# An encoder layer on one core: the tiles that TensorE reads are given the lowest places in SBUF

## The chip, the cores and the metric

The kernel runs on one core of a Trainium2 chip. The metric is the device time of one execution in microseconds (us). Before the change the median of three runs was 736.91 us (736.8 to 738.08). One further execution was profiled; it took 736.86 us, of which 735.1 us lie between its first and its last instruction (the span).

## The reference

One layer over 256 tokens of width 1024, in float32. An RMS norm is followed by one wide projection, four branches (a gated linear recurrence, differential attention, latent attention, retention), a gated merge of the four, an output projection, a squared-ReLU feed-forward of width 4096, and a gated addition of a side input:

```
xn = rms_norm(x, norm1_g)
(a_x, a_g, b_q, b_k, b_v, c_q, c_kv, c_kpe, d_q, d_k, d_v, d_g, gate_logits) = split(xn @ w_in)
y_a, y_b, y_c, y_d = the four branches
gates  = sigmoid(gate_logits + gate_b)
merged = gates[0]*(y_a @ w_br_a) + gates[1]*(y_b @ w_br_b) + gates[2]*(y_c @ w_br_c) + gates[3]*(y_d @ w_br_d)
x = x + merged @ w_out
x = x + square(relu(rms_norm(x, norm2_g) @ w_ff1)) @ w_ff2
x = x + sigmoid(rms_norm(x, norm3_g) @ w_ple_gate) * (p @ w_ple_proj)
```

## The kernel before

**Split products.** Every large product is made of three products of a reduced float32 format (F32R): each operand is split into a high part (a rounded copy) and a low part (the rest), and high by high, high by low and low by high are summed in PSUM (`a_mm`, `mm3`). ScalarE makes the high part and VectorE the low part.

**Weights.** Weight blocks of up to 1 MB are loaded by DMA from the SP queue into three buffers `raw` of 8 KB a partition (`load`, L361). `pieces` (L370) splits them into `hi` and `lo`, each a ring of five buffers of 4 KB a partition (NR = 5). From there TensorE reads them.

**Two forms of product.** In the a form (`a_mode`, L394) the activations are the stationary operand (128x128) and the weights are streamed, 512 columns at a time: `xTh`, `xTl` (the normed input, transposed and split), `y` (the split branch outputs), `h` (the split feed-forward activations), `cT` and `pT` are stationary there. A block of 1024 rows and 512 columns takes 48 matmuls, 24 for each half of the weights. In the b form (`b_mode`, L427) the weights are stationary and 256 columns of `xTh`, `xTl` are streamed; it makes the two inputs of the recurrence and the first feed-forward product. All of these are issued from one line, L194 (`mm`); transposes against the identity come from L207.

**Branch outputs.** `y4()` (L463) hands out the buffers of the split outputs: eight buffers of 4 KB a partition (NY = 8), tile name `y` in the profile. They hold the four branches' outputs in turn (read by `merge`, 96 matmuls for each of the four), the merged sum (read by the `w_out` product, 96 matmuls), the first half of the feed-forward activations (tiles 0 to 7 of 16, read by the `w_ff2` product, 192 matmuls), and at last the weights of the first 512 columns of `w_ple_gate`, where they are the streamed operand against a stationary `xTh` or `xTl` (48 matmuls). The other half of the feed-forward activations lies in the pools `L` and `SH` (tile name `h`).

**Order.** The code is laid out stage by stage; small generators (`side`, `tick`) put the attention and recurrence steps between blocks of the large products, and the tile framework sets the order on each engine from that. The last stages are `merge` of the fourth branch, `w_out`, `w_ple_proj`, 16 blocks of `w_ff1`, `w_ff2`, and the ple gate, which goes over two token halves t and inside each over two column halves c (0: weights in `y`, 1: weights in `hi`, `lo`).

**Places in SBUF.** A pool gets its place when it is opened, one behind the other from 16 KB of each partition on (below that lies a reserved area). Within a pool the tiles follow in the order of their first use. Where the tiles lie, in KB from the start of a partition, as the built program has them:

| tile | before | after |
|---|---|---|
| ident | 29.1 | 16.1 |
| xTh, xTl | 32.4 to 48.4 | 16.6 to 32.6 |
| hi | 73.2 to 93.2 | 32.6 to 52.6 |
| lo | 93.2 to 113.2 | 52.6 to 72.6 |
| y (eight buffers) | 183.2 to 215.2 | 72.6 to 104.6 |
| xs (rows of the input, later the sum) | 16.1 to 24.1 | 104.6 to 112.6 |
| par and other constants | 24.1 to 32.4, 48.4 to 49.2 | 112.6 to 121.2 |
| raw (three buffers) | 49.2 to 73.2 | 121.2 to 145.2 |
| small | 113.2 to 115.2 | 145.2 to 147.2 |
| SH (attention scratch, h 14 and 15, pT) | 115.2 to 147.2 | 147.2 to 179.2 |
| L (attention operands, h 8 to 13, cT) | 147.2 to 183.2 | 179.2 to 215.2 |
| gate | 215.2 to 223.2 | 215.2 to 223.2 |

Before, `ident`, `xs`, `xTh`, `hi`, `lo` and `raw` start at multiples of 64 bytes, and `y`, `SH`, `L` and `gate` at 32 bytes past one. After, `ident`, `xTh`, `xTl`, `hi`, `lo` and `y` start at multiples of 128 bytes; `SH`, `L` and `gate` are still 32 bytes past a multiple of 64.

Of the kernel before, what the change touches and what calls it, by code (L numbers as in the profile page):

```python
# [8 lines left out]
F32 = mybir.dt.float32  # L9
F32R = mybir.dt.float32r  # L10
# [4 lines left out]
P = 128  # L15
S = 256
# [4 lines left out]
NR, NY, NG, NL, NS = 5, 8, 4, 18, 16  # L21
# [146 lines left out]
def encoder_kernel(ctx: ExitStack, tc: tile.TileContext, a, out):  # L168
    nc = tc.nc
    MULT, ADD, SUB, MAX = ALU.mult, ALU.add, ALU.subtract, ALU.max  # L170

    const = ctx.enter_context(tc.tile_pool(name="const", bufs=1))
    ring = ctx.enter_context(tc.tile_pool(name="ring", bufs=4))
    psacc = ctx.enter_context(tc.tile_pool(name="psacc", bufs=4, space=bass.MemoryType.PSUM))
    psmm = ctx.enter_context(tc.tile_pool(name="psmm", bufs=4, space=bass.MemoryType.PSUM))
    small = ctx.enter_context(tc.tile_pool(name="small", bufs=4))
# [49 lines left out]
                nc.sync.dma_start(xs[:, t, w], a['x'][0, t * P:(t + 1) * P, w])  # L226
        nc.sync.dma_start(par[:, :O_LATE], a['params'][:, :O_LATE])

    ident = const.tile([P, P], F32, name="ident")
    make_identity(nc, ident)  # L230
    eps = const.tile([P, 3], F32, name="eps")
    for j, v in enumerate((EPS, 1e-33)):
# [61 lines left out]
        return nhalf[:, :2 * n].rearrange("p (t n) -> p t n", t=2)  # L294


    xTh = const.tile([P, 8, S], F32R, name="xTh")
    xTl = const.tile([P, 8, S], F32R, name="xTl")

    def rstd(src, scratch):  # L300

# [59 lines left out]
    def load(name, r0, n0):  # L361
        o, (_, _, rows, _, nn, mode) = offs[name, r0, n0]
        sz = rows * nn // P
        raw = ring.tile([P, 2048], F32, tag="raw", name="raw", bufs=3)
        with tc.high_priority(AHEAD):
            nc.sync.dma_start(raw[:, :sz], a['weights'][o:o + rows * nn].rearrange("(p c) -> p c", c=sz))
        return raw
# [23 lines left out]
    def a_mode(xh, xl, name, KT, n0, nn, by_token=0):  # L391


        ps = [acc_bank()[:, :nn] for _ in range(2)]  # L394
        held = []
        for k0 in range(0, KT, 4):
            kc = min(4, KT - k0)
            raw = load(name, k0 * P, n0)
            for p0 in range(0, kc, 2):
                kp = min(2, kc - p0)  # L400
                hi, lo = pieces(raw, p0 * nn, kp * nn)
                late = k0 >= KT - by_token
                for t in range(2):
                    for j in range(kp):
                        k = k0 + p0 + j
                        args = (ps[t], t, xh, xl, k, hi, lo, slice(j * nn, (j + 1) * nn), k == 0, k == KT - 1)
                        if late and t == 1:
                            held.append(args)
                        else:
                            a_mm(*args)  # L410
            tick(kc * nn / 2048)
        if held:
            yield ps[0]
            for args in held:
                a_mm(*args)
            yield ps[1]
        else:
            yield ps
# [4 lines left out]
    def b_mode(xh, xl, name, n0):  # L423

        ps = acc_bank().rearrange("p (f s) -> p f s", s=S)
        raw = load(name, 0, n0)
        for f in range(2):  # L427
            hi, lo = pieces(raw, f * 1024, 1024)
            for k in range(8):
                w = slice(k * P, (k + 1) * P)  # L430
                mm(ps[:, f, :], hi[:, w], xh(k), k == 0, False)
                mm(ps[:, f, :], hi[:, w], xl(k), False, False)
                mm(ps[:, f, :], lo[:, w], xh(k), False, k == 7)
        tick(1)
        return ps
# [5 lines left out]
    with tc.tile_pool(name="br", bufs=1) as br:  # L441
# [19 lines left out]
                    split_scaled(xTh[:, kk, :], xTl[:, kk, :], pt[:, k, :], c1('norm1_g', kk))  # L461

        def y4():  # L463
            return br.tile([P, 4, S], F32R, tag="y4", name="y4", bufs=NY)

        def yhl():

            return [[y4(), y4()] for _ in range(2)]
# [554 lines left out]
        for f2 in range(16):  # L1023
            ps = b_mode(xh, xl, 'w_ff1', f2 * 256)
            rl = br.tile([P, 512], F32, tag="gate", name="rl", bufs=NG)
            act(rl, ps.rearrange("p f s -> p (f s)"), AF.Relu)
            tt(rl, rl, rl, MULT)
            if f2 < 8:
                if f2 % 2 == 0:
                    h2 = [x.rearrange("p k s -> p (k s)") for x in (y4(), y4())]  # L1030
                hT.append([x[:, 512 * (f2 % 2):512 * (f2 % 2) + 512] for x in h2])
            elif f2 < 14:
                hT.append([L("h", F32R), L("h", F32R)])
            else:
                hT.append([SH("h").bitcast(F32R), SH("h").bitcast(F32R)])
            split(hT[f2][0], hT[f2][1], rl)
# [14 lines left out]
        for c in range(2):  # L1051
            alloc = (lambda: y4().rearrange("p k s -> p (k s)")) if c == 0 else None
            for k0 in (0, 4):
                raw = load('w_ple_gate', k0 * P, 512 * c)
                held += [pieces(raw, p0 * 512, 1024, alloc) for p0 in (0, 2)]
# [36 lines left out]
```

## Time and profile before

| | |
|---|---|
| median of three runs | 736.91 us |
| profiled execution | 736.86 us |
| its span | 735.1 us |
| TensorE (PE) busy | 718.0 us, 98% of the span, 4066 matmuls |
| weight loads (PEld) busy | 622.7 us, 85% |
| VectorE (DVE) busy | 526.6 us, 72% |
| ScalarE (ACT) busy | 428.2 us, 58% |
| HBM read | 126.74 MB |
| granted TensorE clock | 1.0 |

PE is TensorE's matmuls, PEld its weight loads, which run beside the matmuls. A matmul's row in the profile has a modelled end, so that the rows of neighbours overlap; the pace of a stream of matmuls is read from their starts. In the timeline a row gives the start, the length, the engine, the line, and the tiles written and read; a row x2 is two instructions merged. In the group rows the columns are the line, engine and operation, the tiles out<-in, the shape, the count, the busy time in us, the mean of one in ns, and the idle time of the engine ahead of them.

### The profile page before, as it was taken

How to read it: one execution, taken by the hardware profiler on the slowest of the kernel's cores; microseconds unless marked ns; L12 is line 12 of the kernel's file. 1: busy time of each engine (PE TensorE's matmuls, PEld its weight loads, DVE VectorE, ACT ScalarE, POOL GpSimd, SP SyncE). 2: the span in 40 equal slices, each digit the busy share in tenths (PEclk: the TensorE clock that was granted, in tenths of full speed). 3: DMA queues.
4: the chain of work that ended last, by engine and by line, in shares of the span. 5: the costliest groups of instructions: out<-in, count | busy, mean ns of one | idle time of the engine just before them, and what ended most of it. 6: DMA issues, size and time to landing. Idle time of an engine off the chain costs nothing.

```text
span 735.1 us, 10616 instructions
## 1 busy us (share of the span) xinstructions
PE 718.0 (98%) x4066; PEld 622.7 (85%) x4066; DVE 526.6 (72%) x893; ACT 428.2 (58%) x744; POOL 49.4 (7%) x58
## 2 busy tenths in 40 slices
PE   5999999999999999999999999999999999999997
PEld 4988889997888898888888888877899999888886
DVE  5988978998777879976775778576666666445652
ACT  7589867483745996556544444445755555445551
POOL 0000012222011033110000101000000000000000
PEclk9999999999999999999999999999999999999999
DMA  8754444365344254443555475543564455536611
GB/s 299 263 218 172 171 172 144 119 247 188 122 161 136 91 180 167 170 170 132 186 173 198 163 244 185 199 171 144 179 222 172 173 179 193 202 118 227 233 52 58
DMA packets 22802, 128.47 MB, mean 175 GB/s; under 512 B 2656, under 2 KB 2912, under 8 KB 9440
## 3 DMA queue, kind: packets, MB, share of 16 engines
q1 hardware_dynamic: 22752, 127.80, 48.8%
q8 instruction: 32, 0.52, 0.3%
q14 instruction: 18, 0.15, 0.1%
HBM read 126.74 MB, written 1.05 MB: 174 GB/s over the span
## 4 chain that ended last, share of the span: by engine, by line
PE 64%; DVE 1%; ACT 0%; issue 0%
PE acc L194 57%; PE mm L194 3%; PE mm L207 2%; PE mm L198 1%; ACT hi L191 0%; DVE lo L185 0%; DVE gate L188 0%; DVE pg L185 0%; DVE y L188 0%; DVE xs L185 0%; ACT pg L191 0%
## 5 line engine op out<-in xcount | busy, mean ns | idle before, releaser
L185 DVE TENSOR_TENSOR lo<-raw,hi 128x1024 fp32r<-128x1024 f32 (+3 forms) x226 | 268.3, 1192 | 119.3 <-ACT hi L191 118.8
L191 ACT ACTIVATE hi<-raw 128x1024 fp32r<-128x1024 f32 (+2 forms) x200 | 207.6, 1043 | 194.8 <-PE acc L194 166.0
L194 PE MATMUL acc<-hi,xTh 128*128 128x512 f32 (+3 forms) x376 | 146.3, 389 | 0.0
L194 PE MATMUL acc<-hi,y 128*128 128x512 f32 x448 | 144.5, 398 | 0.0
L194 PE MATMUL acc<-hi,xTl 128*128 128x512 f32 (+3 forms) x376 | 142.8, 380 | 0.0
L194 PE MATMUL acc<-lo,xTh 128*128 128x512 f32 (+3 forms) x376 | 142.6, 379 | 0.0
L194 PE MATMUL acc<-xTl,hi 128*128 128x256 f32 x384 | 109.1, 284 | 0.2 <-DVE xTl L188 0.2
L194 PE MATMUL acc<-xTh,hi 128*128 128x256 f32 x384 | 109.2, 286 | 0.0
L194 PE MATMUL acc<-xTh,lo 128*128 128x256 f32 x384 | 108.7, 284 | 0.0
L194 PEld LDWEIGHTS acc<-hi,y 128*128 128x128 f32 x448 | 84.2, 188 | 19.8
L194 PE MATMUL acc<-lo,y 128*128 128x512 f32 x224 | 89.0, 397 | 0.0
L194 PEld LDWEIGHTS acc<-hi,xTl 128*128 128x128 f32 x376 | 70.6, 188 | 13.1
L194 PEld LDWEIGHTS acc<-hi,xTh 128*128 128x128 f32 x376 | 70.7, 188 | 13.0
L194 PEld LDWEIGHTS acc<-lo,xTh 128*128 128x128 f32 x376 | 70.7, 188 | 12.1
L194 PEld LDWEIGHTS acc<-xTl,hi 128*128 128x128 f32 x384 | 74.0, 193 | 0.7 <-DVE xTl L188 0.5
L194 PEld LDWEIGHTS acc<-xTh,hi 128*128 128x128 f32 x384 | 73.8, 193 | 0.2
L194 PEld LDWEIGHTS acc<-xTh,lo 128*128 128x128 f32 x384 | 73.7, 192 | 0.1
L194 PEld LDWEIGHTS acc<-lo,y 128*128 128x128 f32 x224 | 42.1, 188 | 9.5
L194 PE MATMUL acc<-hi,h 128*128 128x512 f32 x128 | 40.7, 397 | 0.0
L194 PEld LDWEIGHTS acc<-hi,h 128*128 128x128 f32 x128 | 23.9, 188 | 5.6
L194 PE MATMUL acc<-lo,h 128*128 128x512 f32 x64 | 25.3, 395 | 0.0
L194 PE MATMUL acc<-hi,cT 128*128 128x384 f32 (+1 forms) x80 | 24.1, 368 | 0.8 <-ACT cqp L191 0.8
(225 smaller groups left out, 890.0 us busy)
## 6 DMA issues: line engine op xcount, KB each, us to landing
raw<-in_weights_dram SPq DMA_DIRECT2D x104, 1024.0 KB, 4.8
raw<-in_weights_dram SPq DMA_DIRECT2D x6, 512.0 KB, 3.5
raw<-in_weights_dram SPq DMA_DIRECT2D x4, 576.0 KB, 3.7
bd<-in_lru_dram SPq DMA_DIRECT2D x8, 256.0 KB, 5.2
gb<-in_gate_b_dram SPq DMA_DIRECT2D x8, 256.0 KB, 5.0
dec<-in_decay_dram SPq DMA_DIRECT2D x8, 256.0 KB, 5.9
raw<-in_weights_dram SPq DMA_DIRECT2D x2, 768.0 KB, 4.3
raw<-in_weights_dram SPq DMA_DIRECT2D x2, 640.0 KB, 3.6
```

The costliest lines, as they stand in the source:

```text
L185: nc.vector.tensor_tensor(out=o, in0=x, in1=y, op=op)
L191: nc.scalar.activation(o, x, f, **kw)
L194: nc.tensor.matmul(o, lhsT=lhsT, rhs=rhs, start=start, stop=stop)
L198: nc.tensor.matmul(o, lhsT=lhsT, rhs=rhs, start=start, stop=stop, skip_group_check=True)
L207: nc.tensor.transpose(o, x, ident[:x.shape[0], :x.shape[0]])
```

## The change

The tiles that the large products read get pools of their own, opened first: `near` (the identity, `xTh`, `xTl`), `ring` (`hi`, `lo`) and `yring` (the eight buffers of `y`). The constants and the three `raw` buffers (now in a pool of their own) come behind them, then everything else. Sizes, buffer counts and rotations are the same. On every engine, and in the DMA queue, the instructions and the semaphores that they wait for stand in the same order as before; only the addresses differ, as in the table above.

```
+    near = ctx.enter_context(tc.tile_pool(name="near", bufs=1))
+    ring = ctx.enter_context(tc.tile_pool(name="ring", bufs=NR))
+    yring = ctx.enter_context(tc.tile_pool(name="yring", bufs=NY))
     const = ctx.enter_context(tc.tile_pool(name="const", bufs=1))
-    ring = ctx.enter_context(tc.tile_pool(name="ring", bufs=4))
+    raws = ctx.enter_context(tc.tile_pool(name="raws", bufs=3))
     psacc = ctx.enter_context(tc.tile_pool(name="psacc", bufs=4, space=bass.MemoryType.PSUM))
...
-    ident = const.tile([P, P], F32, name="ident")
+    ident = near.tile([P, P], F32, name="ident")
...
-    xTh = const.tile([P, 8, S], F32R, name="xTh")
-    xTl = const.tile([P, 8, S], F32R, name="xTl")
+    xTh = near.tile([P, 8, S], F32R, name="xTh")
+    xTl = near.tile([P, 8, S], F32R, name="xTl")
...
-        raw = ring.tile([P, 2048], F32, tag="raw", name="raw", bufs=3)
+        raw = raws.tile([P, 2048], F32, tag="raw", name="raw", bufs=3)
...
         def y4():
-            return br.tile([P, 4, S], F32R, tag="y4", name="y4", bufs=NY)
+            return yring.tile([P, 4, S], F32R, tag="y4", name="y4", bufs=NY)
```

## The prediction

> **What bounds the kernel now.** I read the page first: how busy each engine is, and the chain that ended last.
>
> ```profile
> PE 718.0 (98%) x4066; PEld 622.7 (85%) x4066; DVE 526.6 (72%) x893; ACT 428.2 (58%) x744; POOL 49.4 (7%) x58
> ...
> PE 64%; DVE 1%; ACT 0%; issue 0%
> PE acc L194 57%; PE mm L194 3%; PE mm L207 2%; PE mm L198 1%; ACT hi L191 0%; DVE lo L185 0%; DVE gate L188 0%; DVE pg L185 0%; DVE y L188 0%; DVE xs L185 0%; ACT pg L191 0%
> ```
>
> TensorE has matmuls under way for 98% of the span, and the chain is its large products. Then the view of the waits, for PE alone: who waited for whom, us in total, times, longest.
>
> ```profile
> PE mm L207 <- DVE xs L452: 8.8, 2, 7.4
> PE mm L207 <- DVE cT L188: 1.4, 1, 1.4
> PE acc L194 <- ACT cqp L191: 0.8, 1, 0.8
> ```
>
> The one long wait is the norm at the start. Behind it TensorE hardly waits for anyone, so the time is the number of matmuls times their pace. The change keeps the number and the order (all engines have the same instructions and the same waits), so only the pace can move.
>
> **The pace, by where the operands lie.** The groups of matmuls of one shape, 128 rows by 512 columns (count, busy us, mean ns):
>
> ```profile
> L194 PE MATMUL acc<-hi,y 128*128 128x512 f32 x448 | 144.5, 398 | 0.0
> L194 PE MATMUL acc<-hi,xTl 128*128 128x512 f32 x328 | 128.0, 390 | 0.0
> L194 PE MATMUL acc<-lo,xTh 128*128 128x512 f32 x328 | 127.8, 390 | 0.0
> L194 PE MATMUL acc<-lo,y 128*128 128x512 f32 x224 | 89.0, 397 | 0.0
> L194 PE MATMUL acc<-hi,h 128*128 128x512 f32 x128 | 40.7, 397 | 0.0
> ...
> L194 PE MATMUL acc<-y,xTh 128*128 128x512 f32 x32 | 10.1, 395 | 0.0
> ...
> L194 PE MATMUL acc<-y,xTl 128*128 128x512 f32 x16 | 6.4, 401 | 0.0
> ```
>
> Those with a `y` or an `h` are some 7 ns longer than those of `xTl` with `hi` or `xTh` with `lo`. In the map of SBUF the short ones have both operands below 114 KB, the long ones have one above it. Since ends are modelled, I take the pace from starts in the timeline. First the fourth gate product (`xT` stationary) and the fourth merge (`y` stationary); four rows, each the first matmul of a stretch or the first one behind it:
>
> ```profile
> 446.71 0.39 PE L194 MATMUL acc<-hi,xTh 128*128 128x512 f32 x1
> ...
> 452.16 0.49 PE L207 MATMUL mm<-ident,dy 128*128 128x128 f32 x3
> ...
> 469.41 0.39 PE L194 MATMUL acc<-hi,y 128*128 128x512 f32 x1
> ...
> 491.80 0.60 PE L207 MATMUL mm<-ident,xs 128*128 128x128 f32 x4
> ```
>
> 24 matmuls with `xT` take 452.16 - 446.71 = 5.45 us, 227.1 ns each. 96 with `y` take 491.80 - 469.41 = 22.39 us, 233.2 ns each. Different stages, though. The ple gate is the better comparison: one stage, the same stationary `xTh` and `xTl`, 24 matmuls with weights from `hi`, `lo`, then 24 with weights held in `y`, then narrower ones:
>
> ```profile
> 713.55 0.40 PE L194 MATMUL acc<-hi,xTh 128*128 128x512 f32 x1
> ...
> 719.02 0.63 PE L194 MATMUL acc<-y,xTh 128*128 128x512 f32 x2
> ...
> 724.63 0.29 PE L194 MATMUL acc<-hi,xTh 128*128 128x256 f32 x1
> ```
>
> 719.02 - 713.55 = 5.47 us, 227.9 ns each; 724.63 - 719.02 = 5.61 us, 233.8 ns each. So a streamed operand high in memory costs 6 ns a matmul, as a stationary one does, and no engine feeds either stretch late: the weights are all held by then.
>
> **What the change moves.** After it `y` lies at 72.6 to 104.6 KB. That is inside the stretch 32 to 113 KB in which both operands now run at 227 ns. Moved into it are 448 + 224 matmuls with `y` stationary and 32 + 16 with `y` streamed, 720 in all.
>
> Of these, 336 stand in long undisturbed stretches: 96 of the fourth merge, 192 of `w_ff2`, 48 of the ple gate. At 233.2 - 227.1 = 6.1 ns by the first pair of stretches and 5.9 by the second, I take 6.0: 336 x 6.0 ns = 2.0 us.
>
> The other 384 (three merges, 288, and `w_out`, 96) come in pieces of about 24 between transposes and attention products, and there the gap is smaller, since the first matmuls of a near stretch run slow too. One piece of each kind:
>
> ```profile
> 200.74 0.48 PE L194 MATMUL acc<-hi,y 128*128 128x512 f32 x1
> ...
> 206.41 0.38 PE L194 MATMUL mm<-bx,baT 128*128 128x128 f32 x2
> ...
> 335.33 0.48 PE L194 MATMUL acc<-hi,xTh 128*128 128x512 f32 x1
> ...
> 340.88 0.49 PE L207 MATMUL mm<-ident,ce 128*128 128x128 f32 x3
> ```
>
> 5.67 us against 5.55 us for 24, so 5.0 ns each: 384 x 5.0 ns = 1.9 us. Together 3.9 us. If all 720 gained 6.1 ns it would be 4.4 us, if all gained 5.0 it would be 3.6.
>
> What stays where it was: `h`, `cT` and `pT` are still high, so half of `w_ff2` and the latent projections keep their 233 ns. The products with `xT` were near already and stay at 227.
>
> **What the move of the other tiles costs.** `raw`, `xs` and the constants go up to 104.6 to 145.2 KB. They are read by ScalarE and VectorE, hardly by TensorE. Rows for the same operation with tiles low and high:
>
> ```profile
> L191 ACT ACTIVATE hi<-raw 128x1024 fp32r<-128x1024 f32 x188 | 199.3, 1063 | 190.5 <-PE acc L194 161.7 <-issue 24.3 <-DMA raw<-in_weights_dram 2.5
> ...
> L191 ACT ACTIVATE xsq<-xs 128x512 f32<-128x512 f32 x12 | 7.6, 631 | 19.5 <-DVE xs L188 9.7 <-DVE xs L185 7.2 <-DMA xs<-in_x_dram 2.6
> ...
> L191 ACT ACTIVATE bsq<-bx 128x512 f32<-128x512 f32 x8 | 5.0, 625 | 0.0
> ...
> L191 ACT ACTIVATE y<-raw 128x1024 fp32r<-128x1024 f32 x4 | 4.1, 1056 | 0.8 <-DMA raw<-in_weights_dram 0.8
> ```
>
> ```profile
> L185 DVE TENSOR_TENSOR lo<-raw,hi 128x1024 fp32r<-128x1024 f32 x210 | 255.5, 1221 | 119.3 <-ACT hi L191 118.8
> ...
> L185 DVE TENSOR_TENSOR rl<-rl 128x512 f32<-128x512 f32 x16 | 10.9, 684 | 0.0
> L185 DVE TENSOR_TENSOR gate<-acc,gb 128x512 f32<-128x512 f32 x16 | 10.5, 682 | 3.0 <-PE acc L194 3.0
> ...
> L185 DVE TENSOR_TENSOR y<-raw,y 128x1024 fp32r<-128x1024 f32 x4 | 4.8, 1222 | 0.5 <-ACT y L191 0.5
> ```
>
> ScalarE squares a low `xs` in 631 ns and a high `bx` in 625; its copy of `raw` takes 1063 ns into a low `hi` and 1056 into a high `y`. VectorE takes 1221 and 1222 ns for a low part written low or high. So these engines don't see the place, and I put the move of `raw` and `xs` at nothing. If ScalarE and VectorE did lose 6 ns an instruction, their slack covers it (72% and 58% busy) except near the start. The view by stretches (busy us and count of PE, PEld, DVE, ACT, POOL) has there:
>
> ```profile
> 20.00:40.00 20.00, 20.00 (x159) 19.66 (x158) 19.66 (x51) 10.10 (x17) 0.00 (x0) 1.00 0.69 252
> ```
>
> VectorE is busy for 19.66 of these 20 us with 51 instructions; a loss of 6 ns on each would be 0.3 us, a gain as much the other way. No row shows a difference, so it is 0, and the 0.3 us lies within the spread below.
>
> **The sum.** 735.1 - 3.9 = 731.2 us of span. The profiled execution has 736.86 - 735.1 = 1.8 us outside it, so 732.9 us; its time is within 0.1 us of the median of 736.91, so no shift is made. By the bounds of the pace it is 732.5 to 733.3. The three runs before spread over 1.3 us, which I add below and above: 731.2 to 734.6.
>
> **A second reading with the same forecast.** The low tiles that TensorE reads start at multiples of 64 bytes before, the high ones 32 bytes past one. After the change `y` starts at a multiple of 128 bytes. So alignment instead of height would make the same 720 matmuls faster by the same amount; the trace of before can't part the two.
>
> **The rivals.**
>
> *No change.* The 6 ns belong to something that goes with those stages and not to the place. For it: products 256 columns wide show no such price. Here the first row has both operands low, the second both high (`L`):
>
> ```profile
> L194 PE MATMUL acc<-xTh,hi 128*128 128x256 f32 x384 | 109.2, 286 | 0.0
> ...
> L198 PE MATMUL mm<-ckn,cqn 128*128 128x256 f32 x48 | 6.6, 288 | 0.0
> ```
>
> 286 and 288 ns are nearly alike, so the price may need the width of 512, or one operand on each side; `y` has both. Against the rival: the ple gate, where stage, stationary operand and shapes are the same and only the streamed tile differs. Time 736.9. The Trainium skill, page "SBUF — State Buffer", section "Who interferes with whom", says that PE and ACT never wait on anyone and makes the shared VectorE and GpSimd port the only point of contention between engines; by that page the change is worth nothing. The 5.47 and 5.61 us in one stage speak against that.
>
> *More than forecast.* All operands at multiples of 128 bytes could free more than `y`: the products with `xT` are not at the best pace that TensorE shows here. The chain in order of time (start, us) has eight matmul instructions of an attention product in plain float32, 256 columns wide, two instructions to a product:
>
> ```profile
> 305.12 1.73 PE mm L194 x8
> ```
>
> That is 216 ns each, the lowest pace of such a length in the trace. If all 512-wide products with `xT` (3 x 328 = 984) went from 227 to 216 and the 720 from 233 to 216, it would be 10.8 + 12.2 = 23 us less, 714 us. For it: the gap of 11 ns exists. Against it: `xTh` at a multiple of 64 and `ident` at one of 128 give no sign of a step, and the 216 ns are of another format and of operands 32 bytes past a multiple of 64. The Trainium skill, page "TensorE: Matmul & The Clock Gate", section "Back-to-back issue gap", gives N / 2.4 + 2.5 ns, which for 512 columns would be an estimate of 215.8 ns; no F32R product of this trace reaches it.
>
> *Slower.* What costs is not height but two operands that TensorE reads at once (the stream, and the next weights) lying close together. Today `xTl` ends 25 KB below `hi`; after the change `xTl`, `hi`, `lo` and `y` lie wall to wall within 88 KB. If closeness decides, the 984 products with `xT` fall to 233 ns and `y` stays there: 984 x 6.0 = 5.9 us more, 742.8 us. It decides from the point at which the first projection's 512-wide stretches run at 233 instead of 227. Against it: `y` lies 70 KB and more from `lo`, about as far as `lo` lies from `xTh` (53 to 81 KB), and only the first pair is slow.
>
> **How the numbers follow.** Forecast 0.80, more 0.06, no change 0.07, slower 0.07. The time of the forecast is 732.9. The range of the forecast, 731.2 to 734.6, leaves out the three rivals, 0.20 together, and is kept. About 0.2% (1.5 us) is what a measurement of this kernel can tell from no change; the forecast and the rival that gains more both end below 735.4, so faster has 0.86, within 0.2% has 0.07 and slower 0.07.
>
> **What would show it.** Right: the group means of `hi,y` and `lo,y` fall from 398 and 397 to about 391, those of `hi,h` stay at 397 and those of `hi,xTl` and `lo,xTh` at 390; the fourth merge takes 21.8 us instead of 22.39; the two stretches of the ple gate are equal at about 5.47 us; the split of `raw` still takes 1063 and 1221 ns. Wrong: `y` still at 233 ns (place doesn't count), `xT` off 227 in either direction (packing or alignment counts), or `y` at 227 and the span not shorter, with new waits on PE for `hi` or `lo` in the merges.

## The result and the profile after

The changed kernel takes 733.29 us (median of six runs, 732.86 to 734.18) against 736.94 us for the kernel before (six runs, 736.71 to 738.17). The ratio is 0.9948 with a 95% interval of 0.9936 to 0.9959. The profiled execution took 732.92 us, with a span of 731.1 us. The time and the rows below came out as forecast; the experiments then showed that the places low in memory were not the cause. (One execution, the first one of f2_after_y32 further down, ran at a granted clock of 0.831 and took 1337.31 us; its time and rows are left out below.)

The page of the changed kernel, busy us and share of the span, and the groups of matmuls that correspond to those of the prediction (the code is five lines longer, so L194 is L199 here):

```profile
PE 714.7 (98%) x4066; PEld 622.6 (85%) x4066; DVE 526.2 (72%) x893; ACT 427.7 (58%) x744; POOL 49.3 (7%) x58
```

```profile
L199 PE MATMUL acc<-hi,y 128*128 128x512 f32 x448 | 142.1, 393 | 0.0
...
L199 PE MATMUL acc<-hi,xTl 128*128 128x512 f32 x328 | 128.0, 390 | 0.0
...
L199 PE MATMUL acc<-lo,y 128*128 128x512 f32 x224 | 87.8, 392 | 0.0
L199 PE MATMUL acc<-hi,h 128*128 128x512 f32 x128 | 40.8, 398 | 0.0
```

The two groups with `y` fell from 398 and 397 ns to 393 and 392. Those of `xTl` stayed at 390, and `h`, which was not to gain, went from 397 to 398. In the timeline the fourth merge, from its first matmul to the first one behind it:

```profile
467.61 0.39 PE L199 MATMUL acc<-hi,y 128*128 128x512 f32 x1
...
489.38 0.38 PE L212 MATMUL mm<-ident,xs 128*128 128x128 f32 x2
```

That is 21.77 us for 96, 226.8 ns each, where it was 22.39 us. The ple gate, whose weights come from `hi`, `lo` first and from `y` then:

```profile
709.80 0.39 PE L199 MATMUL acc<-hi,xTh 128*128 128x512 f32 x1
...
715.24 0.39 PE L199 MATMUL acc<-y,xTh 128*128 128x512 f32 x1
...
720.68 0.28 PE L199 MATMUL acc<-hi,xTh 128*128 128x256 f32 x1
```

Both stretches now take 5.44 us (5.47 and 5.61 before). The splits of `raw`, which moved up, kept their lengths to the nanosecond:

```profile
L196 ACT ACTIVATE hi<-raw 128x1024 fp32r<-128x1024 f32 x188 | 199.3, 1063 | 188.3 <-PE acc L199 156.9 <-issue 26.4 <-DMA raw<-in_weights_dram 2.9
```

```profile
L190 DVE TENSOR_TENSOR lo<-raw,hi 128x1024 fp32r<-128x1024 f32 x210 | 255.4, 1221 | 116.5 <-ACT hi L196 116.0
```

### The profile page after: what moved, and what is told of

It reads as the page before. It is cut to its first block, busy times and chain, and to the rows that moved or that the text cites. A ratio compares the mean times of both kernels' runs of the same rounds, so it can differ in the third digit from the quotient of the medians.

```text
span 731.1 us, 10616 instructions
## 1 busy us (share of the span) xinstructions
PE 714.7 (98%) x4066; PEld 622.6 (85%) x4066; DVE 526.2 (72%) x893; ACT 427.7 (58%) x744; POOL 49.3 (7%) x58
## 4 chain that ended last, share of the span: by engine, by line
PE 64%; DVE 1%; ACT 0%; issue 0%
PE acc L199 57%; PE mm L199 3%; PE mm L212 2%; PE mm L203 1%; ACT hi L196 0%; DVE lo L190 0%; DVE gate L193 0%; DVE pg L190 0%; DVE y L193 0%; DVE xs L190 0%; ACT pg L196 0%
## 5 line engine op out<-in xcount | busy, mean ns | idle before, releaser
L199 PE MATMUL acc<-hi,xTh 128*128 128x512 f32 (+3 forms) x376 | 146.3, 389 | 0.0
L199 PE MATMUL acc<-hi,xTl 128*128 128x512 f32 (+3 forms) x376 | 142.8, 380 | 0.0
L199 PE MATMUL acc<-lo,xTh 128*128 128x512 f32 (+3 forms) x376 | 142.5, 379 | 0.0
L199 PE MATMUL acc<-hi,y 128*128 128x512 f32 x448 | 142.1, 393 | 0.0
L199 PE MATMUL acc<-xTl,hi 128*128 128x256 f32 x384 | 109.2, 285 | 0.2 <-DVE xTl L193 0.2
L199 PE MATMUL acc<-xTh,hi 128*128 128x256 f32 x384 | 109.2, 286 | 0.0
L199 PE MATMUL acc<-xTh,lo 128*128 128x256 f32 x384 | 108.7, 284 | 0.0
L199 PEld LDWEIGHTS acc<-hi,y 128*128 128x128 f32 x448 | 84.1, 188 | 17.5
L199 PE MATMUL acc<-lo,y 128*128 128x512 f32 x224 | 87.8, 392 | 0.0
L199 PEld LDWEIGHTS acc<-hi,xTl 128*128 128x128 f32 x376 | 70.6, 188 | 13.2
L199 PEld LDWEIGHTS acc<-hi,xTh 128*128 128x128 f32 x376 | 70.7, 188 | 12.9
L199 PEld LDWEIGHTS acc<-lo,xTh 128*128 128x128 f32 x376 | 70.8, 188 | 12.2
L199 PEld LDWEIGHTS acc<-xTl,hi 128*128 128x128 f32 x384 | 74.1, 193 | 0.7 <-DVE xTl L193 0.6
L199 PEld LDWEIGHTS acc<-xTh,hi 128*128 128x128 f32 x384 | 73.9, 193 | 0.1
L199 PEld LDWEIGHTS acc<-xTh,lo 128*128 128x128 f32 x384 | 73.8, 193 | 0.1
L199 PEld LDWEIGHTS acc<-lo,y 128*128 128x128 f32 x224 | 42.1, 188 | 8.3
L199 PE MATMUL acc<-hi,h 128*128 128x512 f32 x128 | 40.8, 398 | 0.0
L199 PEld LDWEIGHTS acc<-hi,h 128*128 128x128 f32 x128 | 24.0, 188 | 5.7
L199 PE MATMUL acc<-lo,h 128*128 128x512 f32 x64 | 25.3, 396 | 0.0
L199 PE MATMUL acc<-hi,cT 128*128 128x384 f32 (+1 forms) x80 | 24.2, 369 | 0.8 <-ACT cqp L196 0.8
```

Of the source, the lines that this page charges most:

```text
L199: nc.tensor.matmul(o, lhsT=lhsT, rhs=rhs, start=start, stop=stop)
```

## The experiments

The prediction held that a product is fast when TensorE's operands lie low in memory, and left open that their alignment counts instead. The first four kernels part these two and a third reading (two operands on different sides of a border). All kernels of this section issue the 4066 matmuls in the order of the kernel before, except f1_before_pad224, where 28 of them, between 16 and 20 us, come in another order. Paces below are means of the times from one matmul's start to the next, within runs of one kind and without steps over 260 ns; they are worked out from every start in a trace, and stand together in a table behind the experiments.

**32 bytes ahead of everything (e1_pad32).** All tiles shift together by 32 bytes.

```
+    pad = near.tile([P, 8], F32, name="pad")
+    nc.gpsimd.memset(pad, 0.0)
     ident = near.tile([P, P], F32, name="ident")
```

> The changed kernel with 32 unused bytes ahead of the near tiles, so that ident, xTh, xTl, hi, lo and y start 32 bytes past a multiple of 128 and L, SH and gate at a multiple of 128; heights are the same to 32 bytes. If height decides: as the changed kernel, 733.3 us, 512-wide products with xT and y at 227 ns, with h at 233 to 234. If alignment decides: the 984 products with xT and the 720 with y go to 233 ns (1704 x 6 = 10.2 us more) and those with h, cT and pT (some 336) to 227 (2 us less), 741.5 us. If it is the two operands lying apart: 733.3 us.

Measured: 733.41 us, ratio to before 0.9949 (0.9934 to 0.9964), and `y` at 227.4 ns though it now starts 32 bytes past a multiple of 128. The remainder of the address by itself decides nothing; `h`, now at multiples of 128, is still at 234.

```profile
L199 PE MATMUL acc<-hi,y 128*128 128x512 f32 x448 | 142.1, 393 | 0.0
```

**The kernel before, with 32 bytes behind the weight rings (e2_before_pad32).** The edit is the same line in the pool `small`.

> The kernel before with 32 unused bytes behind the weight rings, so that y, h, L, SH and gate start at multiples of 128 bytes, at the same heights. If height decides: as before, 736.9 us, y and h at 233 ns. If alignment decides: some 1056 products with y, h, cT and pT fall to 227 ns, 1056 x 5.7 = 6 us less, 730.9 us.

Measured: 736.55 us, ratio 0.9996 (0.9987 to 1.0006). `y` and `h` start at multiples of 128 and run at 233.3 ns. So far height stands.

```profile
L194 PE MATMUL acc<-hi,y 128*128 128x512 f32 x448 | 144.6, 398 | 0.0
```

**Everything that TensorE reads put high (e4_all_high).** The order of the pools is turned round, and `br` is opened with them. The lines give the order in which the pools are opened, not the code itself, here and in e5_weights_high.

```
-    near, ring, yring, const, raws, (PSUM), small, br
+    const, raws, small, br, near, ring, yring, (PSUM)
```

> The changed kernel with the order of the pools turned round: everything else first, then ident, xTh, xTl, hi, lo, y at 134.7 to 223.2 KB. If height decides: all 512-wide products run at 233 ns, 984 x 5.5 to 6 = 5.4 to 5.9 us above the kernel before, 742.5 us. If it is two operands on different sides of some border: both are high now, so xT and y run at 227 ns, h (low, with high weights) at 233, and the time is that of the changed kernel, 733 us. The 256-wide products should stay at 120 ns by both.

Measured: 732.2 us, ratio 0.9937 (0.992 to 0.9953), the opposite of what height asks. And `h`, at 66.7 to 126.7 KB with its weights at 151 to 191 KB, is fast too, so a border between the operands falls as well:

```profile
L200 PE MATMUL acc<-hi,y 128*128 128x512 f32 x448 | 142.1, 393 | 0.0
...
L200 PE MATMUL acc<-hi,xTl 128*128 128x512 f32 x328 | 128.0, 390 | 0.0
...
L200 PE MATMUL acc<-hi,h 128*128 128x512 f32 x128 | 39.9, 391 | 0.0
```

All three groups of 512 columns are at 390 to 393 ns, with addresses from 67 to 223 KB.

**Only the weights high (e5_weights_high).**

```
-    near, ring, yring, const, raws, (PSUM), small, br
+    near, yring, const, raws, small, br, ring, (PSUM)
```

> The changed kernel with only hi and lo put high (183.2 to 223.2 KB); ident, xTh, xTl and y stay low (16.1 to 64.6 KB), h lies at 115 to 175 KB. If height of either operand decides: all 512-wide products at 233 ns, 742.5 us. If only the stationary operand's height counts: xT and y stay at 227, 733 us. If two sides of a border decide: xT and y at 233, h with both operands high at 227, 741.4 us. The b form, whose stationary operand is high here, stays at 120 ns if 256-wide products don't feel it; if they do, 1152 x 6 = 6.9 us come on top.

Measured: 738.96 us, ratio 1.0024 (1.0014 to 1.0033). The roles are exchanged, and the b form, which was expected to stay or to get slower, gets faster (first row a form with `y`, then with `xTl`, b form, `h`):

```profile
L200 PE MATMUL acc<-hi,y 128*128 128x512 f32 x448 | 144.5, 398 | 0.0
...
L200 PE MATMUL acc<-hi,xTl 128*128 128x512 f32 x328 | 129.6, 395 | 0.0
...
L200 PE MATMUL acc<-xTl,hi 128*128 128x256 f32 x384 | 108.1, 282 | 0.1
...
L200 PE MATMUL acc<-hi,h 128*128 128x512 f32 x128 | 40.0, 391 | 0.0
```

The same group of the b form in the kernel before:

```profile
L194 PE MATMUL acc<-xTl,hi 128*128 128x256 f32 x384 | 109.1, 284 | 0.2 <-DVE xTl L188 0.2
```

From start to start its feed-forward stage goes from 120.3 to 117.7 ns a matmul. `h` is at 391 and `xTl` at 395. What all six kernels have in common is the distance of the two operands' start addresses modulo 256 bytes. Where it is 0, a 512-wide product runs at 227 ns; where it is 32, 64, 96 or 160, at 233 to 234. In the kernel before, `xT` and the weights both leave 192, but `y` and `h` leave 224. The change happened to give `y` the remainder of the weights, 128, because all tiles ahead of it are multiples of 256 bytes long. That is the new theory; being low is the rival, and the next kernels part the two where they were still mixed.

**The kernel before, nothing moved, 224 bytes of padding (f1_before_pad224).** `y`, `h`, `cT` and `pT` stay at 123 to 215 KB and get the remainder 192.

```
+    pad = small.tile([P, 56], F32, tag="pad", name="pad", bufs=1)
+    nc.gpsimd.memset(pad, 0.0)
     ident = const.tile([P, P], F32, name="ident")
```

> The kernel before, nothing moved, with 224 unused bytes behind the small tiles, so that y, h, cT and pT start at the same remainder of 256 bytes as hi, lo, xTh and xTl (192); they stay at 115 to 223 KB. New theory, relative offset: a 512-wide product runs at 227 ns when its stationary and its streamed operand have the same start modulo 128 or 256 bytes, at 230 to 234 when not. Then y and h and the 512-wide ones of cT and pT fall to 227: 720 x 5.4 + 256 x 6 = 5.4 us less than before, 731.6 us, below the changed kernel. If being low or on one side of a border counts: 737 us, y and h at 233.

Measured: 732.13 us, ratio 0.9939 (0.9925 to 0.9953). The whole gain of the change, without the change:

```profile
L194 PE MATMUL acc<-hi,y 128*128 128x512 f32 x448 | 142.0, 392 | 0.0
...
L194 PE MATMUL acc<-hi,h 128*128 128x512 f32 x128 | 40.0, 391 | 0.0
```

**The changed kernel with y 32 bytes off, y still low (f2_after_y32, profiled again as g4_y32_again).**

```
+    pad = yring.tile([P, 8], F32, tag="pad", name="pad", bufs=1)
+    nc.gpsimd.memset(pad, 0.0)
```

> The changed kernel with 32 unused bytes between lo and y: y stays low (72.7 to 104.7 KB) but starts 32 bytes off the remainder of hi, lo and xT. Relative offset: y back at 233 ns, 733.3 + 3.9 = 737.2 us. If place counts: 733.3 us, y at 227. A side reading: h, cT and pT then stand at 128 modulo 256 from hi and lo; at 227 if the period is 128 bytes, at 233 or more if it is 256 (227 would take 1.5 us off the time).

> The changed kernel with 32 unused bytes between lo and y once more, for a profile at the full clock: 736.7 us, rows of hi and y at 397 to 398 ns, 96 matmuls of the fourth merge in 22.4 us, with y at 72.7 to 104.7 KB. The rows of h, 128 modulo 256 off the weights, at 390 ns if the period is 128 bytes, at 397 and more if it is 256.

Measured: 736.6 us, the median of nine runs, ratio 0.9997 (0.9987 to 1.0006); the execution of g4_y32_again, from which the rows are, took 737.55 us. With `y` at 72.7 to 104.7 KB the gain is gone:

```profile
L199 PE MATMUL acc<-hi,y 128*128 128x512 f32 x448 | 144.5, 398 | 0.0
...
L199 PE MATMUL acc<-hi,h 128*128 128x512 f32 x128 | 40.6, 396 | 0.0
```

The fourth merge runs from 470.05 to 492.44 us, 22.39 us, exactly as in the kernel before. `h`, 128 off, stays slow, so the period is not 128.

**The changed kernel with y 128 bytes off (g3_y128).** The padding is 32 elements instead of 8.

> The changed kernel with 128 unused bytes between lo and y; y is low and 128 bytes off the remainder of hi, lo and xT modulo 256. If the period is 128 bytes: as the changed kernel, 733.3 us, y at 227 ns. If it is 256 or more: y at 230 to 234, 735.5 to 737.5 us. By the sweep (lo at 128 from y: 229 ns, the lowest there, among unequal neighbours) the period of 128 is the likelier.

Measured: 736.98 us, ratio 0.999 (0.9981 to 1.0); `y` at 232.5 ns. The likelier side of the expectation lost: 128 bytes off is nearly as slow as 32. The period is 256: in the kernel before, `xT` and the weights lie 256 apart modulo 512 and are fast.

```profile
L199 PE MATMUL acc<-hi,y 128*128 128x512 f32 x448 | 144.2, 397 | 0.0
```

**One remainder for all (f4_after_pad160).** The changed kernel with 160 bytes in `small`, which gives `h`, `cT` and `pT` the remainder 128 of all others.

> The changed kernel with 160 unused bytes behind the small tiles, so that h, cT and pT get the same remainder as all the rest. Relative offset: h from 234 to 227 ns, 256 x 6.7 = 1.7 us less, 731.6 us. If place counts: 733.3 us, h at 234.

Measured: 732.11 us, ratio 0.9928 (0.9915 to 0.9941); `h` falls from 234.1 to 227.1 ns. Against the changed kernel that is 1.2 us by the medians of two sets of runs, 1.7 expected. It is no better than f1_before_pad224, which leaves `y` high, so the order of the pools adds nothing that these runs can tell.

**Ten buffers at eight remainders (f6_sweep).**

```
-            hi = ring.tile([P, 1024], F32R, tag="hi", name="hi", bufs=NR)
-            lo = ring.tile([P, 1024], F32R, tag="lo", name="lo", bufs=NR)
+            hi = ring.tile([P, 1032], F32R, tag="hi", name="hi", bufs=NR)
+            lo = ring.tile([P, 1032], F32R, tag="lo", name="lo", bufs=NR)
```

> The changed kernel with 32 unused bytes behind each of the ten buffers of hi and lo, so that the ten start at eight different remainders of 256 (steps of 32). One look, to read the pace by offset. Relative offset: in the 512-wide products with xT (remainder 128) the pace depends on the buffer, 227 ns in hi 0 and lo 3 and 230 to 234 in the others; time some 3 to 5 us above the changed kernel. If place counts: all at 227. The b form (256 wide) gives its pace by offset too; where hi and lo lay off xT by 96 it ran at 118 ns against 120.

Measured: 737.85 us in one execution. The expectation held only in part. The `lo` buffer with the remainder of `xT` ran at 228.4 ns and the other four at 231.3 to 232.5, but the `hi` buffer with that remainder ran at 232.1, no better than the rest: the pace of a matmul also hangs on its neighbours, and here `hi` and `lo` of a pair never agree. The b form ran its feed-forward stage at 118.4 ns a matmul. As a map of single offsets the run fails, and it bounds the theory: an equal remainder gave 227 ns only where all products of a stretch had it. The b form as a whole ran faster with mixed remainders (120.3 ns in the kernel before).

**The b form set off by 64 and by 160 bytes (g1_ff1_off64, g2_ff1_off160).** On top of f4_after_pad160, the normed input of the feed-forward is written further on in slightly longer tiles, and only `w_ff1` reads it there. In g2_ff1_off160 both 16 are 40 (elements of 4 bytes); the line that writes the input is left out here.

```
+    xTh_ = near.tile([P, 8 * S + 64], F32R, name="xTh")
+    xTl_ = near.tile([P, 8 * S + 64], F32R, name="xTl")
+    xTh, xTl = (x[:, :8 * S].rearrange("p (k s) -> p k s", s=S) for x in (xTh_, xTl_))
+    fTh, fTl = (x[:, 16:16 + 8 * S].rearrange("p (k s) -> p k s", s=S) for x in (xTh_, xTl_))
...
-            ps = b_mode(xh, xl, 'w_ff1', f2 * 256)
+            ps = b_mode(lambda k: fTh[:, k, :], lambda k: fTl[:, k, :], 'w_ff1', f2 * 256)
```

> The kernel in which everything has one remainder (after_pad160), and xTh, xTl written 64 bytes further on for the first feed-forward product alone (the b form, 768 matmuls, 256 wide, weights stationary). In the sweep and with the weights high that form ran at 117 to 118 ns off the remainder and at 120 on it. Relative offset with an opposite sign for the b form: 768 x 2.5 = 1.9 us less than after_pad160, 730.2 us, feed-forward rows from 120.3 to about 118 ns. If the 118 ns came from something else: 732.1 us.

> As the one before with 160 bytes instead of 64. If any offset off the remainder serves: 730.2 us again; if the size counts the two differ, by up to 768 x 2 = 1.5 us.

Measured: 727.47 us with 64 bytes, ratio 0.9863 (0.9841 to 0.9886), and 731.68 us with 160, ratio 0.9921 (0.9904 to 0.9938). The feed-forward product with 64 bytes, from its first matmul to the first one of `w_ff2`:

```profile
521.98 0.28 PE L199 MATMUL acc<-xTh,hi 128*128 128x256 f32 x1
...
609.45 0.39 PE L199 MATMUL acc<-hi,y 128*128 128x512 f32 x1
```

768 matmuls in 87.47 us, 113.9 ns each. The same in f4_after_pad160:

```profile
521.70 0.28 PE L199 MATMUL acc<-xTh,hi 128*128 128x256 f32 x1
...
614.07 0.40 PE L199 MATMUL acc<-hi,y 128*128 128x512 f32 x1
```

92.37 us, 120.3 ns each. The gain is 4.9 us, more than twice the 1.9 expected. The b form of the first projection, whose input is not shifted, stays at 119.9 ns in the same kernel (120.0 in f4_after_pad160). With 160 bytes the stage takes 91.4 us (521.90 to 613.31), 119.0 ns. So the size of the offset counts here, and 64 is the best of those tried; others were not tried alone. This is the fastest kernel of the study, clear of both the one before and the changed one.

The table gives, for `xT`, `y` and `h`, the distance in bytes (stationary start less streamed start, modulo 256) and the pace of the 512-wide products:

| kernel | xT | y | h | us |
|---|---|---|---|---|
| before | 0: 227.3 | 32: 233.2 | 32: 233.2 | 736.9 |
| after | 0: 227.5 | 0: 227.5 | 96: 234.1 | 733.3 |
| e1_pad32 | 0: 227.5 | 0: 227.4 | 96: 234.2 | 733.4 |
| e2_before_pad32 | 0: 227.4 | 64: 233.3 | 64: 233.3 | 736.6 |
| e4_all_high | 0: 227.5 | 0: 227.5 | 0: 226.9 | 732.2 |
| e5_weights_high | 160: 233.4 | 160: 233.4 | 0: 227.5 | 739.0 |
| f1_before_pad224 | 0: 227.5 | 0: 227.3 | 0: 227.1 | 732.1 |
| g4_y32_again | 0: 227.7 | 32: 233.2 | 128: 232.4 | 737.6 |
| g3_y128 | 0: 227.6 | 128: 232.5 | 224: 233.2 | 737.0 |
| f4_after_pad160 | 0: 227.4 | 0: 227.3 | 0: 227.1 | 732.1 |

Every entry at 0 lies between 226.9 and 227.7, every other between 232.4 and 234.2. In these kernels a distance of 192 occurs only in the ple gate of e2_before_pad32, where `y` is streamed: 44 steps there average 230.2 ns, against 228.6 at 0 in the changed kernel and 233.4 at 224 in the kernel before. On so few steps it is only a hint that the price is not the same at every distance.

## Why the prediction was right in its number and wrong in its reason

**The pace as the only lever.** Right for the change: PE stays at 98% busy, the order of the matmuls is the same, and apart from 0.6 us at the start (below) the time gained lies in the stages whose pace changed.

**"Moved into it are ... 720 in all".** The count was right, and so was the price, 5 to 6 ns. By the stages with `y`, each from its first product with `y` to the first matmul behind its last, the gain is: three merges 0.43 + 0.31 + 0.49 us, the fourth 0.62, `w_out` 0.42, `w_ff2` 0.60 + 0.55, ple gate 0.26; together 3.7 us against 3.9 in the sum. The long stretches gave the 2.0 us forecast, the pieces 1.65 instead of 1.9.

**"That is inside the stretch 32 to 113 KB in which both operands now run at 227 ns".** This is the step that failed. The place was never the cause: f1_before_pad224 has the gain with `y` at 183 KB, f2_after_y32 loses it with `y` at 73 KB. Height and remainder were mixed in the trace of before, since everything behind the small tiles was both high and 32 bytes off. What the runs show in its place is the distance of the two start addresses modulo 256 bytes: 233.2 ns at 32 and 227.5 at 0 for `y`. That the new place of `y` brought this distance to 0 was luck: the reading by place did not ask for it, and 32 bytes of padding undo it.

**"A second reading with the same forecast".** Half right. It named alignment, and the remainder of 128 as what `y` gains; but alignment as such counts for nothing (e1_pad32, e2_before_pad32). The distance between the two operands does.

**"What stays where it was: `h`, `cT` and `pT`".** They stayed slow, but not as they were: their distance went from 32 to 96 bytes, and `h` from 233.2 to 234.1 ns, 192 x 0.9 = 0.2 us lost that no term had. The span fell by 4.0 us all the same (3.7 - 0.2 = 3.5 by these stages). The rest is near the start: the first product begins at 11.74 us instead of 12.38. In the profiles of the eleven other experiments at full clock it begins between 12.06 and 12.74 us, e1_pad32 and g3_y128 with the changed order of the pools among them, so this 0.6 us can't be put down to the change. That the profiled 732.92 us meets the forecast of 732.9 is therefore luck in part; the medians fell by 3.65 us, which is what the stages give.

**The move of `raw` and `xs` at nothing.** Right: 1063 and 1221 ns, as before, and 631 ns for the squares of `xs`.

**The rivals.** No change and slower did not come. The evidence given for no change, 256-wide products alike low and high, was misread: both of those pairs have a distance of 0 modulo 256, so they could not show a price. "Two operands that TensorE reads at once" was the right place to look, under the wrong name: closeness doesn't count, the remainder does. The rival that gains more asked for the 512-wide products with `xT` below 227 ns; no run had that. The N / 2.4 + 2.5 ns that the prediction quotes from the Trainium skill, page "TensorE: Matmul & The Clock Gate", section "Back-to-back issue gap", stands there for an isolated matmul and not for a stream like these. The Trainium skill, page "TensorE: Matmul & The Clock Gate", section "LDWEIGHTS (loading the stationary operand)", gives P / 1.2 ns for a weight load, an estimate of 107 ns for 128 columns; the 113.9 ns of the b form in g1_ff1_off64 stay above it, and no run here shows what lies between.

## What to carry to other kernels

When the same matmul runs at two paces in one trace, compare the start addresses of its two operands modulo 256 bytes before comparing where they lie: some bytes of padding move the pace by 3% at 512 columns and 5% at 256. The sign differs by form here (512 columns are fastest at distance 0, 256 columns with the weights stationary at 64 among the offsets tried), so it has to be tried for each. And a change that moves everything at once tests no single cause: a kernel that only adds padding is the cheapest control.

## What the runs showed of the hardware that was not expected

- In stretches in which all products have the same distance, a 512-wide F32R product with `xT`, `y` or `h` stationary takes 227 ns from start to start when the stationary and the streamed operand start at the same remainder of 256 bytes, and 232.4 to 234.2 ns at distances of 32, 64, 96, 128, 160 and 224, wherever in the partition they lie (16 to 223 KB). With mixed distances (f6_sweep) an equal remainder did not always help: 232.1 ns for one `hi` buffer.
- The 256-wide b form of the feed-forward takes 120.3 ns at distance 0 and 113.9 with the streamed operand 64 bytes further on. With it 160 bytes further on it takes 119.0 in g2_ff1_off160 but 117.7 in e5_weights_high, where the streamed operand starts 96 bytes short of the weights' remainder, which is the same modulo 256. So this distance alone does not fix the pace of the b form.
- Which part of TensorE's reads makes this, and what neighbours with different distances do to each other (f6_sweep), stays open.
